# Hymba-style two-layer trunk: the last token tile's second half of y in two 256-column banks, and its reciprocal root by square root on ScalarE and reciprocal on VectorE

## The chip, the cores and the metric

The program runs on one core of a Trainium2 chip. The metric is device microseconds of one execution; lower is better. Three runs of the kernel before took 316.14 to 316.76 us, with a median of 316.38 us. A separate execution was profiled, and its own time is given below.

## The reference

Two layers work on x, which has 256 tokens (two tiles of 128) and 1024 columns. Each layer computes:

```
mod = silu(c) @ W_ada + b_ada                 -> shift, scale, gate
h   = RMSNorm(x) * (1 + scale) + shift
[q k v g for branch A | q k v g for branch B] = h @ W_in
o_A = dilated sliding-window attention,  o_B = block-sparse attention
y   = RMSNorm([o_A*silu(g_A) | o_B*silu(g_B)] @ W_out)
x   = x + gate * y
```

RMSNorm divides each token's row by the root of its mean square plus 1e-6. So the last thing that the program does, for each token tile of the second layer, is: multiply by W_out, take the mean square over 1024 columns, form its reciprocal root, scale, add to x, and write 128 rows of the result.

## The kernel before

Every float32 operand of a product is split in two parts: a rounded high part (tiles `whi`, `hi`) and the rest (`wlo`, `lo`). A product is then three matrix multiplications: high by high, low by high and high by low. Weights stream from HBM in pieces of 512 KB into a ring of seven buffers (`raw`). ScalarE makes `whi` from a piece (line 205), VectorE makes `wlo` (line 212, one instruction for each 512 columns), and TensorE multiplies with `product` (line 513: 512 columns of weights move past 128 tokens).

The first 60 us or so are a list of steps in a fixed order (`FIRST_STEPS`), which interleaves the first layer's modulation (its weights are multiplied directly, line 414, and the result leaves by line 418), the first norm (lines 702 and 713), the first input products (line 753) and the tables of sines and cosines (`make_rope`, lines 328 to 331). A step `w00` splits one weight piece on ScalarE and VectorE, the step `s00` right behind it multiplies with it, and then `a2` and `b2` multiply modulation weights. After this list only TensorE keeps the order in which the code is written (line 836). The order of the other engines' instructions is chosen by a scheduler, from what each instruction depends on; it may place an instruction ahead of code that stands earlier. Within one engine the queue is then worked off in order.

ScalarE's functions come from tables. Where an instruction needs a function that the loaded table does not hold, an `ACT_TABLE_LOAD` stands in its queue. Square and Copy need none of their own in this program: they run behind Silu, Sin and Exp without one.

The end of a layer for one token tile is `out_product` (which calls `product` for each half `cc` of the 1024 columns and each branch `br`) and `post_norm`. In the last layer's last tile the half `cc` = 0 is finished first (both branches), then `cc` = 1 gets branch 0 and branch 1: 24 matrix multiplications with 512 columns into one PSUM bank. `post_norm` squares each half on ScalarE with a running sum (line 685: an ACTIVATE and a read of the accumulator), multiplies it by the gate on VectorE (line 687), adds the two sums and epsilon on GpSimd (line 464) and raises the sum to the power -0.5 there (line 465). VectorE then scales and adds x for both halves (line 691), and SyncE issues a write for each (line 693).

Of the kernel before, what the change touches and what calls it, by code (L numbers as in the profile page):

```python
# [9 lines left out]
F32 = mybir.dt.float32  # L10
F32R = mybir.dt.float32r
I32 = mybir.dt.int32
AF = mybir.ActivationFunctionType
ALU = mybir.AluOpType
PSUM = bass.MemoryType.PSUM

P = 128
# [3 lines left out]
EPS = 1e-6  # L21
# [53 lines left out]
def trunk(ctx: ExitStack, tc: tile.TileContext, x, c, positions, pre_gain, post_gain,  # L75
          w_ada, b_ada, w_in, w_out, out):
    nc = tc.nc
    B, S, DM = x.shape
    L = w_in.shape[0]
    KT = DM // P  # L80
    KH = KT // 2
    NT = S // P
    CW = 512
# [6 lines left out]
    ap = ctx.enter_context(tc.tile_pool(name="acts", bufs=1))  # L90
    ps = ctx.enter_context(tc.tile_pool(name="psum", bufs=1, space=PSUM))
    start = ExitStack()
# [7 lines left out]
    xs = ap.tile([P, NT, DM], F32, name="xs")  # L100
# [67 lines left out]
    for x in FIRST_LOADS.split():  # L168
        i, g, m = x[0], int(x[1]), int(x[2:] or 0)
        if i in "ab":  # L170
            n = GROUPS[g][1]
# [24 lines left out]
    hi_q, lo_q = {}, {}  # L196
# [25 lines left out]
    ones = cp.tile([P, P], F32, name="ones")  # L222
# [3 lines left out]
    dummy = cp.tile([P, 1], F32, name="dummy")  # L226
# [152 lines left out]
    def ada_sum(l):  # L379

        assert all((l, i) in folded for i in range(KT))
        pm = ps.tile([P, CW], F32, name="o", bufs=1)
        for j in range(4):
            nc.tensor.matmul(pm[32 * j:32 * j + 32, :], ones[:, 0:32], acc[l, 0][:, j * CW:(j + 1) * CW],
                             start=True, stop=True, tile_position=(0, 32 * j))
        part = ap.tile([P, CW], F32, name="hf", bufs=2)
        nc.scalar.activation(part, pm, AF.Copy)
        parts[l] = part

    parts = {}  # L390
# [39 lines left out]
    gate = {}  # L430
# [24 lines left out]
        nc.vector.tensor_mul(gate[l][:, sl], pm, gate[l][:, sl])  # L455


    def rstd_of(ms, other=None):

        e = ap.tile([P, 2], F32, name="rstd", bufs=4)  # L460
        if other is None:
            nc.gpsimd.tensor_scalar(e[:, 0:1], ms, EPS, None, op0=ALU.add)
        else:
            nc.gpsimd.tensor_scalar(e[:, 0:1], ms, other, EPS, op0=ALU.add, op1=ALU.add)
        nc.gpsimd.tensor_tensor(e[:, 1:2], e[:, 0:1], nhalf, op=ALU.pow)
        return e[:, 1:2]
# [9 lines left out]
    def pre_norm(l, t):  # L476
        xn = ap.tile([P, DM], F32, name="oo", bufs=2)
        ms = ap.tile([P, 2], F32, name="ms", bufs=4)
        for cc in range(2):
            sl = slice(cc * CW, (cc + 1) * CW)  # L480
            nc.scalar.activation(xn[:, sl], xs[:, t, sl], AF.Square, scale=1.0 / 32.0, accum_out=ms[:, cc:cc + 1])
        r = rstd_of(ms[:, 0:1], ms[:, 1:2])
        nc.scalar.activation(xn[:, 0:CW], xs[:, t, 0:CW], AF.Copy, scale=r)
        nc.vector.tensor_scalar_mul(xn[:, CW:DM], xs[:, t, CW:DM], r)
        return xn
# [19 lines left out]
    def product(bank, act, t, key, first, last, part=None):  # L505

        if key + (0 if part is None else part,) not in hi_q:
            split_upto(seq.index(key) + 1)
        ahi, alo = act
        for k in range(KH) if part is None else (2 * part, 2 * part + 1):  # L510
            whi, wlo = hi_q[key + (k // 2,)], lo_q[key + (k // 2,)]
            for i, (a, w) in enumerate(((ahi, whi), (alo, whi), (ahi, wlo))):
                nc.tensor.matmul(bank, a[:, k, t, :], w[:, k % 2, :], start=first and k + i == 0,  # L513
                                 stop=last and k == KH - 1 and i == 2)
# [16 lines left out]
    qk, vv, gs, qkT, oo = {}, {}, {}, {}, {}  # L531
# [120 lines left out]
    oT = {}  # L652
# [19 lines left out]
    yb = {}  # L672

    def out_product(l, t, cc, br):
        if br == 0:
            yb[t, cc] = ps.tile([P, CW], F32, name="mm", bufs=3)
        assert ready_o[br] == KH
        product(yb[t, cc], oT[br], t, ("out", l, cc, br), br == 0, br == 1)

    def post_norm(l, t, last):  # L680
        ms = ap.tile([P, 4], F32, name="ms2", bufs=2)
        sq = ap.tile([P, NT, CW], F32, name="qk", bufs=3)[:, 0, :]
        yg = ap.tile([P, DM], F32, name="oo", bufs=2)
        for cc in range(2):
            nc.scalar.activation(sq, yb[t, cc], AF.Square, scale=1.0 / 32.0, accum_out=ms[:, cc:cc + 1])  # L685
            sl = slice(cc * CW, (cc + 1) * CW)
            nc.vector.tensor_mul(yg[:, sl], yb.pop((t, cc)), gate[l][:, sl])  # L687
        r = rstd_of(ms[:, 0:1], ms[:, 1:2])
        for cc in range(2):
            sl = slice(cc * CW, (cc + 1) * CW)  # L690
            nc.vector.scalar_tensor_tensor(xs[:, t, sl], yg[:, sl], r, xs[:, t, sl], op0=ALU.mult, op1=ALU.add)
            if last:
                nc.sync.dma_start(out[0, t * P:(t + 1) * P, sl], xs[:, t, sl])
# [75 lines left out]
    def sub_in(l, ci, hf, t, part=None):  # L769
        if l == 0 and part is not None:  # L770
            ready(t, 4 * hf + 2 * part + 1)
        begin = hf == 0 or (l, ci) == (0, 5) and len(parked) > 0
        if (l, ci, t) not in mm:
            tag = "mm" if (l, ci) != (0, 2) else ("s", "t")[t]
            mm[l, ci, t] = ps.tile([P, CW], F32, name=tag, bufs=3 if tag == "mm" else 2)
        if CH[ci] % 4 == 3:
            gate_product(mm[l, ci, t], hT[l, hf], t, ("in", l, ci, hf), hf)
        else:
            product(mm[l, ci, t], hT[l, hf], t, ("in", l, ci, hf), begin, hf == 1, part)
        if hf == 1 and part != 0:  # L780
            evac(l, ci, t)

    seq = list(loads)
    spl = [0]

    def split_upto(n):
        while spl[0] < min(n, len(seq)):
            split_half(seq[spl[0]])
            for a in ADA_AT.get(spl[0], []):
                ada_step(a)  # L790
            spl[0] += 1
# [9 lines left out]
    for step in FIRST_STEPS.split():  # L801
        i, g, m = step[0], int(step[1]), int(step[2:] or 0)
# [38 lines left out]
    for l in range(L):  # L841
        nxt = l + 1 < L
        slots = []
        if l > 0:
            slots += [(0, 0, 0), (0, 1, 0), (1, 0, 0), (1, 1, 0), (0, 0, 1), (0, 1, 1), (1, 0, 1), (1, 1, 1)]
        for ci in range(2, 8):
            if l > 0 or ci != 2 and not (ci == 5 and parked):
                slots += [(ci, 0, 0), (ci, 0, 1)]
            slots += [(ci, 1, 0), (ci, 1, 1)]
        side = {}  # L850

        def at(i, f, *a):
            side.setdefault(i, []).append((f, a))
        for p in range(4):
            for br, o in ((0, AT_A[l]), (1, AT_B[l])):
                d = OS[l], OX[l], OV[l]
                at(o + 2 * p, st_T, br, p)
                at(o + d[0] + 2 * p, st_S, br, p)
                at(o + d[1] + 2 * p, st_X, br, p)
                at(o + d[2] + 2 * p, st_V, br, p)  # L860
        for p in range(4):
            at(AO[l] + AO2[l] * p // 2, finish, 0, p)
        at(GATE_AT[l], gate_begin, l)
        for h in range(2):
            at(GATE_AT[l] + GATE_D[l] + h, gate_end, l, h)
        if l > 0:
            for g in range(2):
                at(H_AT[g], make_h, l, 1, xn0[1], (g,))
        for n, (ci, hf, t) in enumerate(slots):
            i = n + 32 - len(slots)  # L870
            split_upto(seq.index(("in", l, ci, hf)) + AHEAD[l])
            sub_in(l, ci, hf, t)
            for f, a in side.get(i, []):
                f(*a)
        base = seq.index(("out", l, 0, 0))
        split_upto(base + 2)
        out_product(l, 0, 0, 0)
        for i in range(32, 42):
            for f, a in side.get(i, []):
                f(*a)  # L880
        out_product(l, 0, 1, 0)
        split_upto(base + 4)
        if nxt:
            ada_sum(l + 1)
        out_product(l, 0, 0, 1)
        if nxt:
            ada_mod(l + 1)
        out_product(l, 0, 1, 1)
        post_norm(l, 0, not nxt)
        if nxt:  # L890
            xn0[0] = pre_norm(l + 1, 0)
        for cc, br in (((0, 0), (1, 0), (0, 1)) if nxt else ((0, 0), (0, 1), (1, 0))):
            out_product(l, 1, cc, br)
        if nxt:
            split_upto(base + 6)
            make_h(l + 1, 0, xn0[0])
        out_product(l, 1, 1, 1)
        post_norm(l, 1, not nxt)
        if nxt:
            xn0[1] = pre_norm(l + 1, 1)  # L900


# [26 lines left out]
```

## Time and profile before

| What | Value |
| --- | --- |
| Runs, median (lowest to highest) | 316.38 us (316.14 to 316.76) |
| Profiled execution: own time, span | 316.34 us, 314.3 us |
| TensorE, share of the span | 94% |
| VectorE, ScalarE, GpSimd | 78%, 65%, 4% |
| Granted TensorE clock, mean over the span | 0.997 of full speed |

The span runs from the first to the last profiled instruction, so 2.04 us of the profiled execution lie outside it. Busy shares are means over stages with different limits. The chain of waits follows the work that ended last back to the start, and says for each moment which engine the end was waiting for. In the rows, PE is TensorE, PEld its weight load, ACT ScalarE, DVE VectorE, POOL GpSimd and SP SyncE; a q behind a name is that engine's sequencer.

### The profile page before, as it was taken

What the parts mean: (1) busy time and instruction counts of PE and PEld (TensorE: products, weight loads), DVE (VectorE), ACT (ScalarE), POOL (GpSimd) and SP (SyncE); (2) the same over time, 40 slices, a digit from 0 to 9 for tenths busy, and PEclk for the clock granted to TensorE, in tenths of its full rate; (3) what the DMA queues carried; (4) which work ended last, traced back from release to release, by engine and by line L of the source; (5) the groups of instructions that cost most, each with busy time, mean ns of one, the idle gap of its engine ahead of it and who ended that gap; (6) DMA issues with size and microseconds to landing.
All of it is one profiled execution on the core that took longest, in us unless ns stands there. A gap on an engine that the chain in (4) does not pass through costs nothing.

```text
span 314.3 us, 5293 instructions
## 1 busy us (share of the span) xinstructions
PE 295.7 (94%) x1817; PEld 237.5 (76%) x1817; DVE 245.4 (78%) x637; ACT 203.9 (65%) x435; POOL 12.4 (4%) x46
## 2 busy tenths in 40 slices
PE   0889999989999999999999999999999999999992
PEld 0666576868777799997787788777777799997881
DVE  4775974999999999989589999979965566776122
ACT  3645363969597569988387385598775579984100
POOL 3100001000010000000021200000000000000001
PEclk9999999999999999999999999999999999999998
DMA  7999999999888877787937649987844441000011
GB/s 248 339 360 355 346 349 283 325 375 302 286 284 291 291 262 246 211 282 242 325 133 232 217 154 340 341 317 239 252 150 136 136 137 64 2 1 2 0 67 67
DMA packets 37394, 70.63 MB, mean 225 GB/s; under 512 B 2492, under 2 KB 12790, under 8 KB 37368
## 3 DMA queue, kind: packets, MB, share of 16 engines
q1 hardware_dynamic: 36960, 69.22, 65.8%
q10 hardware_dynamic: 408, 1.09, 0.9%
q8 instruction: 14, 0.23, 0.3%
q14 instruction: 12, 0.10, 0.1%
HBM read 69.24 MB, written 1.05 MB: 224 GB/s over the span
## 4 chain that ended last, share of the span: by engine, by line
PE 83%; DVE 5%; DMA 4%; ACT 3%; issue 1%; POOL 1%; SPq 1%; ACTq 0%; DVEq 0%; POOLq 0%
PE mm L513 41%; PE mm L526 15%; PE o L642 4%; PE mm L753 4%; PE t L625 4%; PE t L513 3%; DVE wlo L212 2%; PE t L571 2%; DMA raw<-in_w_ada_dram 2%; PE o L414 2%; PE s L592 2%; PE s L595 2%; DMA rows<-in_b_ada_dram 2%; PE s L753 1%; ACT whi L205 1%
## 5 line engine op out<-in xcount | busy, mean ns | idle before, releaser
L212 DVE TENSOR_TENSOR wlo<-raw,whi 128x512 fp32r<-128x512 f32 x160 | 102.3, 688 | 6.5 <-PE mm L513 3.6
L205 ACT ACTIVATE whi<-raw 128x1024 fp32r<-128x1024 f32 (+1 forms) x88 | 84.2, 979 | 24.8 <-DMA raw<-in_w_in_dram 10.5
L513 PE MATMUL mm<-whi,hi 128*128 128x512 f32 x200 | 81.7, 408 | 0.0
L513 PE MATMUL mm<-wlo,hi 128*128 128x512 f32 x200 | 79.1, 395 | 0.0
L513 PE MATMUL mm<-whi,lo 128*128 128x512 f32 x200 | 79.0, 395 | 0.0
L513 PEld LDWEIGHTS mm<-whi,hi 128*128 128x128 f32 x200 | 37.6, 188 | 10.4 <-issue 1.7
L513 PEld LDWEIGHTS mm<-wlo,hi 128*128 128x128 f32 x200 | 37.6, 188 | 8.8
L513 PEld LDWEIGHTS mm<-whi,lo 128*128 128x128 f32 x200 | 37.7, 189 | 8.1 <-DVE lo L502 0.3
L526 PE MATMUL mm<-hi,whi 128*128 128x256 f32 x128 | 37.2, 291 | 0.0
L526 PE MATMUL mm<-hi,wlo 128*128 128x256 f32 x128 | 36.1, 282 | 0.0
L526 PE MATMUL mm<-lo,whi 128*128 128x256 f32 x128 | 36.0, 281 | 0.0
L604 ACT ACTIVATE z<-z,den 128x128 f32<-128x128 f32 x64 | 28.3, 447 | 5.0 <-DVE den L601 4.9
L526 PEld LDWEIGHTS mm<-hi,whi 128*128 128x128 f32 x128 | 24.1, 188 | 1.2 <-issue 0.2
L526 PEld LDWEIGHTS mm<-lo,whi 128*128 128x128 f32 x128 | 24.2, 189 | 0.2
L526 PEld LDWEIGHTS mm<-hi,wlo 128*128 128x128 f32 x128 | 24.1, 188 | 0.0
L364 DVE SCALAR_TENSOR_TENSOR acc_g<-raw,cs,acc_g 128x1024 f32<-128x1024 f32 x16 | 20.6, 1284 | 2.8 <-DMA raw<-in_w_ada_dram 2.7
L687 DVE TENSOR_TENSOR oo<-mm,gate 128x512 f32<-128x512 f32 x8 | 5.5, 690 | 17.8 <-ACT qk L685 17.7
L685 ACT ACTIVATE qk<-mm 128x512 f32<-128x512 f32 x8 | 4.7, 592 | 21.9 <-PE mm L513 21.9
L364 DVE SCALAR_TENSOR_TENSOR acc_ss<-raw,cs,acc_ss 128x1024 f32<-128x1024 f32 x14 | 17.6, 1275 | 0.0
L628 ACT ACTIVATE pT<-t 128x384 f32<-128x384 f32 x32 | 14.0, 493 | 0.1
L642 PE MATMUL o<-pT,vv 128*64 128x128 f32 x192 | 14.0, 281 | 0.0
L625 PE MATMUL t<-ident,z 128*128 128x128 f32 x96 | 13.6, 277 | 0.0
(173 smaller groups left out, 450.6 us busy)
## 6 DMA issues: line engine op xcount, KB each, us to landing
raw<-in_w_in_dram SPq DMA_DIRECT2D x64, 512.0 KB, 5.3
raw<-in_w_ada_dram SPq DMA_DIRECT2D x32, 512.0 KB, 5.0
raw<-in_w_ada_dram SPq DMA_DIRECT2D x32, 256.0 KB, 6.0
raw<-in_w_out_dram SPq DMA_DIRECT2D x16, 512.0 KB, 4.9
xs<-in_x_dram SPq DMA_DIRECT2D x2, 512.0 KB, 4.3
gate<-in_post_norm_gain_dram ACTq DMA_DIRECT2D x2, 512.0 KB, 5.2
out_dram<-xs SPq DMA_DIRECT2D x4, 256.0 KB, 2.1
rows<-in_b_ada_dram ACTq DMA_DIRECT2D x2, 8.0 KB, 5.3
```

The lines of the kernel that those rows point to most:

```text
L205: nc.scalar.activation(hi_q[key][:, a:b, :], raw[:, a:b, :], AF.Copy)
L212: nc.vector.tensor_sub(lo[:, d, :], raw[:, d, :], hi[:, d, :].bitcast(F32))
L364: nc.vector.scalar_tensor_tensor(a[:, sl], r[:, sl], cs[:, k:k + 1], a[:, sl], op0=ALU.mult, op1=ALU.add)
L414: nc.tensor.matmul(pm[32 * j:32 * j + 32, :w], csz[:, k, :], r[:, i * w:(i + 1) * w], start=k < 4, stop=k >= 4, tile_position=(0, 32 * j))
L513: nc.tensor.matmul(bank, a[:, k, t, :], w[:, k % 2, :], start=first and k + i == 0, stop=last and k == KH - 1 and i == 2)
L526: nc.tensor.matmul(bank[:, b * S:(b + 1) * S], w[:, k % 2, c0:c0 + P], a[:, k].rearrange("p t q -> p (t q)"), start=hf + b + k + i == 0, s ...
L571: nc.tensor.transpose(pt[:, (2 * i + t) * P:(2 * i + t + 1) * P], qk[br, i][:, t, p * P:(p + 1) * P], ident)
L604: nc.scalar.activation(z[:, a:b], z[:, a:b], AF.Exp, bias=den[:, 0, t, i:i + 1], scale=-1.0, accum_out=den[:, 1, t, i:i + 1])
L625: nc.tensor.transpose(pt[:, b * P:(b + 1) * P], pp[i][:, b * P:(b + 1) * P], ident)
L628: nc.scalar.activation(d, pt[:, :NS], AF.Copy)
L642: nc.tensor.matmul(ob[i * HD:(i + 1) * HD, q0:q0 + P], v[:, t, h], res[i][:, c0:c0 + P], start=t == 0, stop=n != 1, tile_position=(0, i * HD))
L753: nc.tensor.matmul(mm[0, ci, t], a[:, k, t, :], w[:, ci, :], start=q == 0 and j == 0 and i == 0, stop=q == 3 and j == 1 and i == 2)
```

## The change

Only the last token tile of the last layer is touched. Its second half of y goes to two PSUM banks of 256 columns each (`last_product`), by 48 matrix multiplications with 256 columns in place of 24 with 512; the first 256 columns are complete 12 multiplications ahead of the others. `last_norm` squares and gates three parts (512, 256 and 256 columns). GpSimd adds the first two sums and then epsilon; ScalarE takes the square root of the third sum with this as its bias; VectorE forms the reciprocal. The power on GpSimd goes. A square root of a constant into a tile that nothing reads (`dummy`) stands ahead of the squares in the code.

```diff
-    def rstd_of(ms, other=None):
+    def rstd_of(ms, other=None, last=False):
-        e = ap.tile([P, 2], F32, name="rstd", bufs=4)
+        e = ap.tile([P, 3], F32, name="rstd", bufs=4)
+        if last:
+            nc.gpsimd.tensor_scalar(e[:, 0:1], ms, EPS, None, op0=ALU.add)
+            nc.scalar.activation(e[:, 2:3], other, AF.Sqrt, bias=e[:, 0:1])
+            nc.vector.reciprocal(e[:, 1:2], e[:, 2:3])
+            return e[:, 1:2]
...
+    def last_product(l, t, br):
+        if br == 0:
+            yb[t, 1] = [ps.tile([P, CW], F32, name="s", bufs=2) for _ in range(2)]
...
+        for c in range(2):
+            for k in range(KH):
+                whi, wlo = hi_q[key + (k // 2,)], lo_q[key + (k // 2,)]
+                for i, (a, w) in enumerate(((ahi, whi), (alo, whi), (ahi, wlo))):
+                    nc.tensor.matmul(yb[t, 1][c][:, :H], a[:, k, t, :], w[:, k % 2, c * H:(c + 1) * H],
+                                     start=br + k + i == 0, stop=br == 1 and k == KH - 1 and i == 2)
...
+    def last_norm(l, t):
...
+        parts = [(yb[t, 0], 0, CW), (yb[t, 1][0][:, :H], CW, CW + H), (yb[t, 1][1][:, :H], CW + H, DM)]
+        nc.scalar.activation(dummy, ones[:, 0:1], AF.Sqrt)
+        for n, (y, a, b) in enumerate(parts):
+            nc.scalar.activation(sq[:, 0:b - a], y, AF.Square, scale=1.0 / 32.0, accum_out=ms[:, n:n + 1])
+            nc.vector.tensor_mul(yg[:, a:b], y, gate[l][:, a:b])
+            if n == 1:
+                nc.gpsimd.tensor_tensor(ms[:, 3:4], ms[:, 0:1], ms[:, 1:2], op=ALU.add)
+        r = rstd_of(ms[:, 3:4], ms[:, 2:3], True)
+        for cc in range(2):
+            sl = slice(cc * CW, (cc + 1) * CW)
+            nc.vector.scalar_tensor_tensor(xs[:, t, sl], yg[:, sl], r, xs[:, t, sl], op0=ALU.mult, op1=ALU.add)
+            nc.sync.dma_start(out[0, t * P:(t + 1) * P, sl], xs[:, t, sl])
```

The queues show where the scheduler put the new instructions. Lines behind the inserted code have higher numbers in the changed kernel: 702, 713 and 726 are 743, 754 and 767 there. First ScalarE's queue near the start of the program, before: the second tile's first norm (`acc_ss`), the copies of transposed x, then a modulated part of h (`hi`), the sines and cosines, and the weight piece of step `w00` (128x1024).

```order
L702 ACTIVATE acc_ss,ms<-xs 128x1024
L713 ACTIVATE acc_g<-t 128x512 x2
...
L726 ACTIVATE hi<-hf 128x128 x2
L328 ACTIVATE sine<-sm 128x2x8
L329 ACTIVATE sine<-sm 128x2x8
L330 ACTIVATE cose<-sm 128x2x8
L331 ACTIVATE cose<-sm 128x2x8
L205 ACTIVATE whi<-raw 128x1024
```

The same two places now:

```order
L743 ACTIVATE acc_ss,ms<-xs 128x1024
L709 ACT_TABLE_LOAD
L709 ACTIVATE dummy<-ones 128x1
L754 ACTIVATE acc_g<-t 128x512 x2
...
L767 ACTIVATE hi<-hf 128x128 x2
L328 ACT_TABLE_LOAD
L328 ACTIVATE sine<-sm 128x2x8
L329 ACTIVATE sine<-sm 128x2x8
L330 ACTIVATE cose<-sm 128x2x8
L331 ACTIVATE cose<-sm 128x2x8
L205 ACTIVATE whi<-raw 128x1024
```

The square root of the constant depends on nothing but a constant, and stands at the start of the program instead of ahead of the last squares. It brings a table load, and the sines and cosines behind it bring another.

Then the end of ScalarE's queue, before: the last attention output and the four squares of the two tiles.

```order
L667 ACTIVATE hi<-oo 128x256 [waits DVE_49]
L685 ACTIVATE qk,ms_3517<-mm 128x512 [waits PE_49]
L685 ACTIVATE qk,ms_3517<-mm 128x512 [waits PE_49,Activation_49]
L685 ACTIVATE qk,ms_3581<-mm 128x512 [waits PE_49]
L685 ACTIVATE qk,ms_3581<-mm 128x512 [waits PE_49,Activation_49]
```

The same place now:

```order
L726 ACTIVATE qk,ms_3517<-mm 128x512 [waits PE_49,Activation_49]
L711 ACTIVATE qk,ms_3606<-mm 128x512 [waits PE_49]
L711 ACTIVATE qk,ms_3606<-s 128x256 [waits PE_49,Activation_49] x2
L463 ACT_TABLE_LOAD [waits Activation_49]
L463 ACTIVATE rstd<-ms_3606,rstd 128x1 [waits Pool_49]
```

Behind the last square there is now a table load, and then the square root. On VectorE a reciprocal of 128x1 follows, ahead of the two last additions; and one weight split in the first layer's attention changes places with its neighbours.

## Rows read from the trace of the kernel before

**Rows 1.** The page: shares of the chain of waits by engine.

```profile
PE 83%; DVE 5%; DMA 4%; ACT 3%; issue 1%; POOL 1%; SPq 1%; ACTq 0%; DVEq 0%; POOLq 0%
```

**Rows 2.** Chain of waits, its end: start us, us, what.

```profile
288.26 19.81 PE mm L513 x84
...
308.16 0.60 ACT qk L685
...
308.94 0.30 POOL rstd L464
...
309.92 0.75 DVE xs L691
```

**Rows 3.** Timeline, the end: start us, us, engine, line, operation [idle before it].

```profile
307.66 0.40 PE L513 MATMUL mm<-wlo,hi 128*128 128x512 f32 x1
...
308.65 0.19 ACT L685 ACTIVATION_READ_ACCUMULATOR qk<-mm 128x1 f32 x1
308.88 0.69 DVE L687 TENSOR_TENSOR oo<-mm,gate 128x512 f32<-128x512 f32 x1 [4.97 <-ACT qk L685]
...
309.32 0.56 POOL L465 TENSOR_TENSOR rstd<-rstd,nhalf 128x1 f32<-128x1 f32 x1
```

**Rows 4.** Chain of waits, unbroken runs of 512-column and of 256-column multiplications.

```profile
237.51 5.58 PE mm L513 x24
...
277.30 5.76 PE mm L526 x48
```

**Rows 5.** Groups by line and form: busy us, mean ns of one, idle before.

```profile
L561 ACT ACT_TABLE_LOAD x4 | 5.1, 1283 | 0.1
L650 ACT ACTIVATE oo<-o 128x256 f32<-128x256 f32 x13 | 4.9, 378 | 0.1
L685 ACT ACTIVATE qk<-mm 128x512 f32<-128x512 f32 x8 | 4.7, 592 | 21.9 <-PE mm L513 21.9
L608 DVE RECIPROCAL rc<-den 128x4 f32<-128x4 f32 x16 | 2.8, 175 | 4.2 <-ACT z L604 4.2
```

**Rows 6.** Timeline, ScalarE around a table load.

```profile
280.16 0.51 ACT L612 ACTIVATE z<-z,rc 128x256 f32<-128x256 f32 x1 [0.25 <-DVE rc L608]
280.69 1.28 ACT L561 ACT_TABLE_LOAD   x1
281.98 0.60 ACT L561 ACTIVATE gs<-mm 128x512 f32<-128x512 f32 x1
```

**Rows 7.** Timeline, ScalarE at the first place near the start.

```profile
9.29 0.19 ACT L702 ACTIVATION_READ_ACCUMULATOR acc_ss<-xs 128x1 f32 x1
10.70 0.60 ACT L713 ACTIVATE acc_g<-t 128x512 f32<-128x512 f32 x1 [1.22 <-PE t L712]
11.55 0.60 ACT L713 ACTIVATE acc_g<-t 128x512 f32<-128x512 f32 x1 [0.26 <-PE t L712]
```

**Rows 8.** Timeline, ScalarE, VectorE and TensorE at the second place near the start.

```profile
18.93 0.57 ACT L726 ACTIVATE hi<-hf 128x128 fp32r<-128x128 f32 x2 [0.54 <-DVE hf L724]
...
19.40 0.20 ACT L328 ACTIVATE sine<-sm 128x16 f32<-128x16 f32 x1
...
19.83 1.04 ACT L205 ACTIVATE whi<-raw 128x1024 fp32r<-128x1024 f32 x1
...
20.28 1.91 DVE L212 TENSOR_TENSOR wlo<-raw,whi 128x512 fp32r<-128x512 f32 x3
...
21.86 0.39 PE L513 MATMUL s<-whi,hi 128*128 128x512 f32 x1
...
23.35 2.32 PE L414 MATMUL o<-raw,csz 128*32 128x512 f32 x16
```

**Rows 9.** Timeline, SyncE: the last loads for those multiplications of line 414.

```profile
16.96 1.00 SPq L136 DMA_DIRECT2D raw<-in_w_ada_dram  x2
```

**Rows 10.** The instructions of line 136: from issue to landing.

```profile
DMA to landing us min/median/max: 4.0/6.0/6.6
```

**Rows 11.** Timeline, TensorE: the same 16 multiplications of the next group.

```profile
47.09 1.92 PE L414 MATMUL o<-raw,csz 128*32 128x512 f32 x16
```

More of the change, by code (lines that the diff above doesn't have):

```diff
@@ L678, in out_product @@
         product(yb[t, cc], oT[br], t, ("out", l, cc, br), br == 0, br == 1)
+    def last_product(l, t, br):
+        if br == 0:
+            yb[t, 1] = [ps.tile([P, CW], F32, name="s", bufs=2) for _ in range(2)]
+        key = ("out", l, 1, br)
+        if key + (0,) not in hi_q:
+            split_upto(seq.index(key) + 1)
+        ahi, alo = oT[br]
+        H = CW // 2
+        for c in range(2):
[5 more added lines that the diff above has]
+    def last_norm(l, t):
+        ms = ap.tile([P, 4], F32, name="ms2", bufs=2)
+        sq = ap.tile([P, NT, CW], F32, name="qk", bufs=3)[:, 0, :]
+        yg = ap.tile([P, DM], F32, name="oo", bufs=2)
+        H = CW // 2
+        parts = [(yb[t, 0], 0, CW), (yb[t, 1][0][:, :H], CW, CW + H), (yb[t, 1][1][:, :H], CW + H, DM)]
[10 more added lines that the diff above has]
+            nc.sync.dma_start(out[0, t * P:(t + 1) * P, sl], xs[:, t, sl])
     def post_norm(l, t, last):
@@ L892, in trunk @@
         for cc, br in (((0, 0), (1, 0), (0, 1)) if nxt else ((0, 0), (0, 1), (1, 0))):
-            out_product(l, 1, cc, br)
+            if nxt or cc == 0:
+                out_product(l, 1, cc, br)
+            else:
+                last_product(l, 1, br)
         if nxt:
@@ L896, in trunk @@
             make_h(l + 1, 0, xn0[0])
-        out_product(l, 1, 1, 1)
-        post_norm(l, 1, not nxt)
-        if nxt:
+            out_product(l, 1, 1, 1)
+            post_norm(l, 1, False)
             xn0[1] = pre_norm(l + 1, 1)
+        else:
+            last_product(l, 1, 1)
+            last_norm(l, 1)
 _INS = ["x", "c", "positions", "pre_norm_gain", "post_norm_gain", "w_ada", "b_ada", "w_in", "w_out"]
```

## The prediction

> **What bounds the kernel now.** I read the page's shares of the chain of waits first. TensorE holds 83% of it, and no other engine more than 5% [rows 1]; so what delays TensorE anywhere delays the end, unless a later wait swallows it. Then I read the end of the chain: 84 multiplications in an unbroken run from 288.26 us, then the square on ScalarE at 308.16, the two instructions on GpSimd from 308.94, and VectorE's scaling at 309.92 [rows 2]. Everything between TensorE's last multiplication, which ends at 307.66 + 0.40 = 308.06 [rows 3], and 309.92 stands alone on the path: 1.86 us in which one engine works at a time. That is what the change rebuilds. What lies behind 309.92 (two additions, two writes) is the same in both kernels. Third I read the timeline at the places near the start where the queue shows new table loads, because there too the reader is to ask who waits behind ScalarE.
>
> **The end, part by part.** The 24 multiplications with 512 columns become 48 with 256. An unbroken run of 24 with 512 columns took 5.58 us and one of 48 with 256 columns, elsewhere in the kernel, 5.76 us [rows 4]. So TensorE ends 0.18 later, at 308.24.
>
> ScalarE started its square 0.10 behind TensorE's end (308.06 to 308.16), and I keep that: 308.34. The square of 512 columns and its accumulator read were over at 308.65 + 0.19 = 308.84, which is 0.68 behind its start [rows 2, 3]. No square of 256 columns is in the trace. From PSUM, a copy of 256 columns took 378 ns and the square of 512 took 592 ns [rows 5]; I take the difference, 0.21, off: the third square is done at 308.34 + 0.47 = 308.81. The bounds are the square of 512 unchanged (0.68) and the copy without any read behind it (0.38).
>
> Now comes the table load of the square root. It stands behind the last square in a queue that is worked off in order, and it waits for that square itself, so nothing covers it. The one at 280.69 began 0.02 behind the end of the instruction ahead of it, took 1.28, and the next instruction began 0.01 later [rows 6]; the mean of its group is 1283 ns [rows 5]. So it runs from 308.83 to 310.11. The square root of 128x1 is not in the trace either; a sine of 128x16 took 0.20 [rows 8], and I take that: 310.12 to 310.32. Its bounds are that 0.20 and the 0.38 of the copy of 256 columns. VectorE starts 0.04 behind ScalarE (308.84 to 308.88 [rows 3]): 310.36. A reciprocal of 128x4 took 175 ns [rows 5], and with 0.03 to the next instruction VectorE scales at 310.56, against 309.92 before: 0.64 later.
>
> Of the work that was taken out, the power on GpSimd (0.56 [rows 3]) and the sum ahead of it (0.30 [rows 2]) go from the path. GpSimd's two new sums need only the first two squares. The middle square starts when the first 256 columns are ready, 12 multiplications or 1.44 us ahead of the end (12 of 5.76 / 48), at about 306.9, and is done at 307.4; two sums of 0.30 with gaps of 0.1 are over by 308.2, long before the square root wants them at 310.1. VectorE's product with the gate for the last 256 columns starts when the third square is done, as the one at 308.88 did [rows 3], and at no more than the 0.69 of 512 columns ends by 309.6; it is covered too. Without the load the same sum would end at 309.27, 0.65 earlier than before: the load alone turns a gain into a loss.
>
> Here a page of the Trainium skill bears: "ScalarE: Activation LUTs", section "What ACT_TABLE_LOAD costs", gives 1283 ns for the load, which the rows share, and about as much again for a drain at each switch, 2.66 us in all. The trace has no such second part beside the load at 280.69; by the page the sum of the end would be near 2.0 us later instead of 0.64. I leave it as a rival below.
>
> **The start, part by part.** The square root of a constant was placed at the start. Its load falls behind the accumulator read that ends at 9.48, where ScalarE was idle for 1.22 us until 10.70 [rows 7]. Load and dummy: 9.50 to 10.78, then about 0.1 to 0.2 for the dummy, so the copy that began at 10.70 begins near 10.9. The next copy waited for TensorE until 11.55 with 0.26 of idle time ahead of it [rows 7], and still starts then. This place costs nothing: the cover is ScalarE's own wait.
>
> The second place is tighter. The sines need their table again, and the load starts behind the pair that ends at 18.93 + 0.57 = 19.50 [rows 8]: 19.52 to 20.80, first sine 20.81 instead of 19.40, all behind it 1.41 later. Behind it stands the split of the weight piece of step `w00`: it ran from 19.83 to 20.87, now from 21.24 to 22.28. TensorE wanted it at 21.86 [rows 8], so 0.99 of the delay is covered and the first of six multiplications starts near 22.32. Its third and sixth also need VectorE's two splits of that piece. The three splits from 20.28 took 1.91 [rows 8], so one follows the other by 0.61 and the last lasts 0.69; now the two start at 22.31 and 22.92 and end at 22.99 and 23.61. At 0.233 for each multiplication (5.58 / 24) the six start at 22.32, 22.55, 23.03, 23.26, 23.50 and 23.73; the sixth stood at 21.86 + 5 x 0.233 = 23.02 before. TensorE is 0.71 late.
>
> Part of that is given back at once. The 16 multiplications of line 414 that follow took 2.32 us from 23.35 [rows 8], and the same 16 of the next group 1.92 [rows 11]: 0.40 of the first was a wait for weights. The last two loads were issued between 16.96 and 17.96 [rows 9], and such a load lands 6.0 us after its issue in the median [rows 10], at 23.0 to 24.0. Starting at 23.35 + 0.71 = 24.06, TensorE finds them there: 24.06 + 1.92 = 25.98 against 23.35 + 2.32 = 25.67. I take 0.31 late. From there on the chain is TensorE behind TensorE, or an engine that waits for TensorE, and I see no wait that gives it back.
>
> SyncE's queue is behind this too: the buffer of that weight piece comes free 1.4 later, and so does the load that waits for it. The loads already issued keep the DMA engines busy meanwhile, so I take nothing for it. The bounds of the start are 0 (a later wait for weights swallows the rest) and 1.41 (the late loads pass the whole delay on).
>
> The exchange of one weight split with its neighbours on VectorE changes no sum of work; I take 0, with 0.1 either way.
>
> **Sum.** The profiled execution took 316.34 us, of which 314.3 was span: 316.34 + 0.64 + 0.31 = 317.29, that is 317.3. The median of the runs is 316.38, so about 0.9 us or 0.3% slower.
>
> **The rivals.**
>
> 1. The start costs nothing in the end: a wait for weights that I can't see in TensorE's chain takes up the 0.31. Time 316.34 + 0.64 = 316.98. For it: such a wait already takes 0.40 of the 0.71. Against it: behind 25.67 the chain hardly leaves TensorE.
>
> 2. The delay of the start is passed on in full, through the buffer that comes free late. Between 0.71 and 1.41 instead of 0.31: 317.7 to 318.4. For it: a load is issued only when a buffer of the ring is free. Against it: a load lands 6 us after its issue, so several are on their way at any time.
>
> 3. The other side, not slower: the load at the end is hidden, because ScalarE fetches the table while it waits for TensorE ahead of the last square. Then the end gains 0.65 and the time is 316.34 - 0.65 + 0.31 = 316.0, or 315.7 with nothing lost at the start. It decides from the point where more than half of the 1.28 is hidden. For it: ScalarE is idle most of the last 20 us. Against it: the load waits for the square itself, and the load at 280.69 started behind the instruction ahead of it and not earlier [rows 6].
>
> 4. A switch of tables costs twice its load, as a drain of the same length would make it: 1.28 more at the end and 1.28 more at the second place of the start, where no cover is left: 317.29 + 2.56 = 319.9. The skill's page above has this rule. Against it: no gap of that size stands around the load at 280.69 [rows 6].
>
> **How the numbers follow.** The forecast has 58%, rival 1 18%, rival 2 13%, rival 3 8% (5% at 316.0, 3% at 315.7), rival 4 3%. A measurement of this kernel can tell about 0.2% from no change, 0.63 us: slower is above 317.01, faster below 315.75. The forecast's own range is 317.2 to 317.7 (the square 0.09 shorter or 0.21 longer, the root up to 0.18 longer). With rival 1 and the lower half of rival 2 the range is 316.8 to 317.9. Slower: 58 + 13 + 3 = 74%; same: 18 + 5 = 23%; faster: 3%. Since the forecast lies only 0.28 above the bound of slower, I move two points, one to each of the others: 72, 24 and 4%.
>
> **What would show it.** At the end of the changed profile: a table load of 1.28 directly behind the last accumulator read, on the chain of waits, and the first scaling some 2.3 us behind TensorE's last multiplication instead of 1.86. At the start: the second load near 19.5, the first multiplication of `s00` near 22.3, and the 16 of line 414 in about 1.9 instead of 2.32, ended near 26.0. TensorE's last multiplication then ends about 0.49 later than before, 0.31 from the start and 0.18 from the narrower tiles. I am wrong if the load is missing from the chain, and the start is wrong if that end is no later than the 0.18 of the narrower tiles.

## The result, and the profile after

| | Median (lowest to highest), runs | Profiled execution, span |
| --- | --- | --- |
| Before | 316.64 us (316.14 to 316.76), 6 | 316.34 us, 314.3 us |
| After | 318.50 us (317.39 to 319.34), 6 | 318.35 us, 316.3 us |

The ratio is 1.0058, with a 95% interval of 1.0045 to 1.0072: slower by 1.4 to 2.3 us. The forecast was slower by 0.95 us, 317.3 in a range that ended at 317.9. The direction was right, the size about half.

**The end.** This is the end of the chain of waits after, which answers to [rows 2] (start us, us, what).

```profile
303.77 5.71 PE s L698 x48
...
309.56 0.48 ACT qk L711 x2
...
310.12 1.28 ACT L463
311.40 0.32 ACTq L970
...
311.94 0.75 DVE xs L718
```

The table load stands on the chain, whole. And these are TensorE, ScalarE, VectorE and GpSimd in the timeline of the same stretch after, which answers to [rows 3] (start us, us, engine, line, operation, and in brackets the idle time before it).

```profile
308.98 0.22 POOL L462 TENSOR_SCALAR rstd<-ms 128x1 f32<-128x1 f32 x1
...
309.19 0.28 PE L698 MATMUL s<-wlo,hi 128*128 128x256 f32 x1
309.56 0.38 ACT L711 ACTIVATE qk<-s 128x256 f32<-128x256 f32 x1 [0.95 <-PE s L698]
309.85 0.19 ACT L711 ACTIVATION_READ_ACCUMULATOR qk<-s 128x1 f32 x1
310.07 0.43 DVE L712 TENSOR_TENSOR oo<-s,gate 128x256 f32<-128x256 f32 x1 [1.00 <-ACT qk L711]
310.12 1.28 ACT L463 ACT_TABLE_LOAD   x1
311.41 0.29 ACT L463 ACTIVATE rstd<-ms,rstd 128x1 f32<-128x1 f32 x1
311.74 0.16 DVE L464 RECIPROCAL rstd<-rstd 128x1 f32<-128x1 f32 x1 [1.24 <-ACT rstd L463]
```

GpSimd has the sum ready by 309.20 (308.98 + 0.22) and VectorE the gated product by 310.50, but the root runs at 311.41 only, behind the load. TensorE's last multiplication ends at 309.47 (309.19 + 0.28) and VectorE scales at 311.94: 2.47 us, against 1.86 before.

**The start.** ScalarE after, at the place of [rows 7].

```profile
8.70 0.19 ACT L743 ACTIVATION_READ_ACCUMULATOR acc_ss<-xs 128x1 f32 x1
8.91 1.28 ACT L709 ACT_TABLE_LOAD   x1
10.20 0.20 ACT L709 ACTIVATE dummy<-ones 128x1 f32<-128x1 f32 x1
10.31 1.25 ACT L754 ACTIVATE acc_g<-t 128x512 f32<-128x512 f32 x2
```

This execution is ahead of the one before here (the read stood at 9.29), since TensorE's first transposition (line 275), which in the kernel before waits for a load, began at 7.32 here and at 7.90 there. So times near the start must be read against their spread: in the seven profiles in which the ring has seven buffers and the split of `w00` is on time, the first 16 multiplications of line 414 end between 25.03 and 25.67, and the next 16 between 48.73 and 49.33. ScalarE and TensorE after, at the place of [rows 8]:

```profile
18.82 0.57 ACT L767 ACTIVATE hi<-hf 128x128 fp32r<-128x128 f32 x2 [0.84 <-DVE hf L765]
19.40 1.28 ACT L328 ACT_TABLE_LOAD   x1
20.70 0.22 ACT L328 ACTIVATE sine<-sm 128x16 f32<-128x16 f32 x1
...
21.14 1.04 ACT L205 ACTIVATE whi<-raw 128x1024 fp32r<-128x1024 f32 x1
...
22.23 0.50 PE L518 MATMUL s<-whi,hi 128*128 128x512 f32 x1 [0.62 <-ACT whi L205]
...
24.09 1.92 PE L414 MATMUL o<-raw,csz 128*32 128x512 f32 x16
```

The 16 multiplications take 1.92 instead of 2.32 and end at 26.01 instead of 25.67 [rows 8]: 0.34 late, as the prediction had it (0.31). But by the end of the next group of 16 [rows 11], at 49.97 instead of 49.01, the delay is 0.96. It grows between, at the next eight multiplications of line 414. TensorE there before, and after:

```profile
32.51 1.12 PE L414 MATMUL o<-raw,csz 128*32 128x512 f32 x8
```

```profile
32.95 1.65 PE L414 MATMUL o<-raw,csz 128*32 128x512 f32 x8
```

SyncE's queue shows what came late. The load of line 126 goes into the buffer of the piece that step `w00` splits. SyncE before, and after:

```profile
22.26 0.34 SPq L126 DMA_DIRECT2D raw<-in_w_in_dram  x1
24.44 0.37 SPq L121 DMA_DIRECT2D raw<-in_w_in_dram  x1
24.91 2.64 SPq L136 DMA_DIRECT2D raw<-in_w_ada_dram  x4
```

```profile
23.57 0.34 SPq L126 DMA_DIRECT2D raw<-in_w_in_dram  x1
25.18 0.37 SPq L121 DMA_DIRECT2D raw<-in_w_in_dram  x1
25.65 1.76 SPq L136 DMA_DIRECT2D raw<-in_w_ada_dram  x2
```

That load is issued 1.31 later, and the loads behind it in the queue, which bring the weights of line 414, 0.74 later. The DMA view of the stretch from 20 to 30 us says whether the loads issued earlier covered that, before and after:

```profile
DMA packets 2354, 3.59 MB, mean 359 GB/s; under 512 B 151, under 2 KB 1584, under 8 KB 2352
```

```profile
DMA packets 1937, 3.18 MB, mean 318 GB/s; under 512 B 130, under 2 KB 1167, under 8 KB 1935
```

They did not: 0.41 MB fewer were moved in the same 10 us, which at 359 GB/s is 1.1 us of transfers. Most of it is missing in two microseconds: from 26 to 28 us the DMA engines moved 0.39 MB, against 0.70 before.

**The middle.** One more difference lies at the boundary of the layers, where GpSimd adds epsilon for the second tile and VectorE waits for the result. GpSimd and VectorE in the timeline before, then after:

```profile
173.97 2.49 DVE L212 TENSOR_TENSOR wlo<-raw,whi 128x512 fp32r<-128x512 f32 x4
...
174.91 1.04 POOL L464 TENSOR_SCALAR rstd<-ms 128x1 f32<-128x1 f32 x1 [2.30 <-ACT oo L481]
...
176.91 0.48 DVE L484 TENSOR_SCALAR oo<-xs,rstd 128x512 f32<-128x512 f32 x1 [0.45 <-POOL rstd L465]
```

```profile
174.96 2.50 DVE L212 TENSOR_TENSOR wlo<-raw,whi 128x512 fp32r<-128x512 f32 x4
...
175.90 1.72 POOL L469 TENSOR_SCALAR rstd<-ms 128x1 f32<-128x1 f32 x1 [2.31 <-ACT oo L486]
...
178.30 0.49 DVE L489 TENSOR_SCALAR oo<-xs,rstd 128x512 f32<-128x512 f32 x1 [0.85 <-POOL rstd L470]
```

The same instruction, begun 0.94 behind the start of VectorE's four splits in both, lasts 1.04 in one and 1.72 in the other. VectorE goes on 1.39 late (176.91 to 178.30), 0.43 more than the 0.96 of the start.

**The ledger of the two profiles.** 0.34 at the start, 0.62 from there to 34 us, 0.43 at the layers' boundary, 0.10 for the narrower tiles (48 with 256 columns in 5.71 us, 24 with 512 in 5.6), and 0.61 behind TensorE make 2.10; the spans differ by 2.0, and some 0.07 is given back between the boundary and the last product.

### The profile page after: what moved, and what is told of

The parts are those of the page before. It is cut to its first block, busy times and chain, and to the rows that moved or that the text cites. A ratio compares the mean times of both kernels' runs of the same rounds, so it can differ in the third digit from the quotient of the medians.

```text
span 316.3 us, 5351 instructions
## 1 busy us (share of the span) xinstructions
PE 297.5 (94%) x1841; PEld 238.9 (76%) x1841; DVE 245.8 (78%) x639; ACT 208.5 (66%) x442; POOL 12.4 (4%) x46
## 4 chain that ended last, share of the span: by engine, by line
PE 84%; DVE 6%; ACT 5%; issue 2%; POOL 1%; ACTq 1%; DVEq 0%; POOLq 0%
PE mm L518 39%; PE mm L531 15%; PE o L647 4%; PE t L630 4%; DVE wlo L212 3%; PE mm L794 3%; PE t L518 3%; PE o L414 3%; PE t L576 2%; PE s L597 2%; PE s L698 2%; PE s L600 2%; ACT whi L205 1%; PE s L518 1%; PE s L794 1%
## 5 line engine op out<-in xcount | busy, mean ns | idle before, releaser
L518 PE MATMUL mm<-whi,hi 128*128 128x512 f32 x192 | 78.5, 409 | 0.0
L518 PE MATMUL mm<-wlo,hi 128*128 128x512 f32 x192 | 75.9, 395 | 0.0
L518 PE MATMUL mm<-whi,lo 128*128 128x512 f32 x192 | 75.8, 395 | 0.0
L518 PEld LDWEIGHTS mm<-whi,hi 128*128 128x128 f32 x192 | 36.1, 188 | 10.1 <-issue 1.7
L518 PEld LDWEIGHTS mm<-wlo,hi 128*128 128x128 f32 x192 | 36.1, 188 | 8.4
L518 PEld LDWEIGHTS mm<-whi,lo 128*128 128x128 f32 x192 | 36.2, 189 | 7.7 <-DVE lo L507 0.3
L647 PEld LDWEIGHTS o<-pT,vv 128*64 128x64 f32 x192 | 10.1, 136 | 4.3 <-issue 2.0
L584 DVE TENSOR_TENSOR qkl<-t,qkh 128x384 fp32r<-128x384 f32 x16 | 8.9, 555 | 5.1 <-ACT qkT L583 4.9
```

The source lines that it names most:

```text
L584: nc.vector.tensor_sub(lo, pt[:, P:], hi.bitcast(F32))
L647: nc.tensor.matmul(ob[i * HD:(i + 1) * HD, q0:q0 + P], v[:, t, h], res[i][:, c0:c0 + P], start=t == 0, stop=n != 1, tile_position=(0, i * HD))
```

## The experiments

The theory, A in the texts: the end costs what was forecast, and the start costs more, because the split of `w00` stands behind a table load and its buffer comes free late, so that loads queued on SyncE come late (A1 where that part of A is meant alone). The rivals are told in the texts with their numbers: that the end or the table loads themselves cost more than forecast, wherever they stand. Each ratio is to the kernel before on the same chip.

### The end without the early load

```diff
-        nc.scalar.activation(dummy, ones[:, 0:1], AF.Sqrt)
```

> The change without its idle square root near the start: no table load there, the load at the end stays. Theory A (the excess over the forecast arises at the start, passed on by late weight loads): only the end is left, 0.6 to 0.75 us over before, about 317.3 us. Theory B (the load at the end costs more than its 1.28 us): the end holds most of the 1.85, about 318.1 us or more.

Measured: 316.78 us against 316.24, ratio 1.0019 (1.0007 to 1.0031), some 0.6 us. The end is the same as in the changed kernel, 2.47 us behind TensorE's last multiplication, and the 16 and 8 multiplications of line 414 take 2.26 and 1.15, as before. So the rebuilt end costs about 0.6 us, and the rest of the loss hangs on the line that was taken out.

### The early load alone, in the kernel before

```diff
+        if last and t == 1:
+            nc.scalar.activation(dummy, ones[:, 0:1], AF.Sqrt)
```

> The kernel before with nothing but the idle square root of a constant: two table loads near the start, the end as it was. Theory A: 1.0 to 1.3 us over before, about 317.8 us, with TensorE waiting for weights of line 414 near 33 us. Theory B: 0.3 us over before, about 316.9 us.

Measured: 317.94 us against 316.24, ratio 1.0043 (1.0021 to 1.0066), 1.36 us by the ratio (0.66 to 2.09), which leaves out theory B's 0.3. A load of a table that no one uses at the start, with nothing changed at the end (1.86 us), costs more than the whole new end. The timeline of its TensorE shows the wait openly:

```profile
33.38 1.05 PE L414 MATMUL o<-raw,csz 128*32 128x512 f32 x4
34.81 1.05 PE L414 MATMUL o<-raw,csz 128*32 128x512 f32 x4 [0.37 <-DMA raw<-in_w_ada_dram]
```

and the list of what its weight loads waited for between 30 and 36 us (us in total, times, longest) names the load:

```profile
PEld o L414 <- DMA raw<-in_w_ada_dram: 1.3, 1, 1.3
```

Its SyncE issued the load of line 126 at 24.04 and those of line 136 from 26.11, and from 20 to 30 us it moved 3.01 MB. The two parts add up within their intervals: 0.60 and 1.36 make 1.96, against 1.84 by the ratio of the first comparison and 2.09 by that of the next run.

### The changed kernel once more

No edit.

> The changed kernel once more, for a second profile and more times: its six times spread over 1.95 us, those of before over 0.62. Theory A: about 318.5 us in the median with the same spread, and the profile shows the delay differing from the first one's between 20 and 50 us and at the layers' boundary, while the end (first scaling 2.46 us behind TensorE's last multiplication) is the same to 0.05. Theory B: the end differs.

Measured: 318.37 us against 316.24, ratio 1.0066 (1.0044 to 1.0088). The loss repeats, and the end is 2.47 again. In this profile the eight multiplications of line 414 took 2.09 (32.73 to 34.82) instead of the 1.65 above: how long TensorE waits there varies from one execution to the next, and the runs of the changed kernel spread over 2 us. The list of waits from 30 to 36 us names the load here too; for the 1.65 above it names nothing ("issue", 0.8 us in two pieces).

```profile
PEld o L414 <- DMA raw<-in_w_ada_dram: 0.9, 1, 0.9
```

### The warm-up held back to the last squares

The square root of a constant becomes one of the first square's sum, so that it cannot be placed before it; its load then stands between the first square and the second.

```diff
-        nc.scalar.activation(dummy, ones[:, 0:1], AF.Sqrt)
...
             nc.vector.tensor_mul(yg[:, a:b], y, gate[l][:, a:b])
+            if n == 0:
+                nc.scalar.activation(dummy, ms[:, 0:1], AF.Sqrt)
```

> The change with the idle square root fed by the first square's sum, so that its load stands between the first and the second square, where ScalarE is idle for some 4 us. Both theories: no load at the start, the one at the end covered; the first scaling 1.15 us behind TensorE's last multiplication instead of 2.46, and 0.55 to 0.65 us under before, about 316.0 us. If a load could not be covered, 317.3 us as without the idle square root.

Measured: 315.84 us against 316.24, ratio 0.9987 (0.9973 to 1.0001). The first scaling comes 1.19 us behind TensorE's last multiplication. Both parts of the loss are gone with one line; the interval just reaches no change, so it was run again below.

### The sines behind the split

The steps `w00` and `s00` are moved ahead of `R2`, which holds the sines. All table loads stay.

```diff
-g02 R2 l11 g03 p02 w00 s00 a2 b2 m2
+g02 l11 g03 p02 w00 s00 R2 a2 b2 m2
```

> The changed kernel with the step of the sines (R2) moved behind steps w00 and s00, so that the second table load of the start runs in ScalarE's idle time. All table loads stay. Theory A (the start's cost comes from the split of w00 that stands behind that load): the start is as before and only the end is left, 0.55 us over before, about 316.8 us; TensorE reaches the first multiplication of s00 near 21.9 us. Theory C (the cost comes from the first of the two loads, or from their number): about 1.9 us over before, as the changed kernel.

Measured: 317.04 us against 316.49, ratio 1.0016 (1.0006 to 1.0027). ScalarE now has the split first and the load behind it:

```profile
19.40 1.05 ACT L205 ACTIVATE whi<-raw 128x1024 fp32r<-128x1024 f32 x1
20.47 1.28 ACT L328 ACT_TABLE_LOAD   x1
```

SyncE issues line 126 at 22.23 as before (22.26), and the eight multiplications take 1.06. Of the loss, only what the kernel without the early load also has is left (1.0019 there). So a load near the start costs nothing that these intervals, some 0.5 us wide to either side, can show where the split does not stand behind it: theory C, by which the loads cost by themselves (1.9 us), falls. The run does not tell TensorE's direct delay from the late loads; the ring below does.

### Two banks, the power kept

The early load goes, and GpSimd forms the reciprocal root by power as before.

```diff
-        nc.scalar.activation(dummy, ones[:, 0:1], AF.Sqrt)
...
-        r = rstd_of(ms[:, 3:4], ms[:, 2:3], True)
+        r = rstd_of(ms[:, 3:4], ms[:, 2:3])
```

> The change with its two banks and three squares, but with the power on GpSimd as before and no square root. Forecast from the parts measured: TensorE 0.10 later, square and accumulator read 0.20 shorter: the first scaling 1.65 us behind TensorE's last multiplication, about 0.1 us under before. If a third square or the two banks cost by themselves: 0.2 us or more over before.

Measured: 316.55 us against 316.49, ratio 0.9997 (0.9987 to 1.0006). The scaling comes 1.70 behind TensorE, 0.16 less than before, and the narrower tiles cost 0.10: no change that can be told, as the sum says. The long form of GpSimd's instruction at the layers' boundary appears here too, without any early load:

```profile
175.23 1.72 POOL L469 TENSOR_SCALAR rstd<-ms 128x1 f32<-128x1 f32 x1 [2.31 <-ACT oo L486]
```

### One bank, the root on ScalarE, its load covered

The last tile keeps one bank of 512 columns; square root and reciprocal as changed; the warm-up behind the first square.

```diff
-        parts = [(yb[t, 0], 0, CW), (yb[t, 1][0][:, :H], CW, CW + H), (yb[t, 1][1][:, :H], CW + H, DM)]
+        parts = [(yb[t, 0], 0, CW), (yb[t, 1], CW, DM)]
...
-        r = rstd_of(ms[:, 3:4], ms[:, 2:3], True)
+        r = rstd_of(ms[:, 0:1], ms[:, 1:2], True)
```

> One bank of 512 columns as before, but square root on ScalarE and reciprocal on VectorE, with the table load covered behind the first square. TensorE as before; square and read 0.68, root 0.30, reciprocal 0.20 and the gaps: the first scaling 1.35 us behind TensorE's last multiplication instead of 1.86, about 0.5 us under before. If root and reciprocal without a load were worth nothing: equal to before.

Measured: 316.31 us against 316.49, ratio 0.9994 (0.9982 to 1.0007). The tail is 1.55 us, and the expectation missed it by 0.20. The end of its chain of waits names what it left out:

```profile
308.22 0.70 ACT qk L710 x2
...
308.94 0.69 DVE oo L711
309.63 0.08 DVE rstd L464
...
309.74 0.75 DVE xs L717
```

VectorE's product with the gate, over 512 columns, stands in its queue ahead of the reciprocal and ends behind the root. It was covered by the two GpSimd instructions before; with a shorter root it is what ends last. The second bank shortens it (0.43 for 256 columns), so the two halves of the change are worth more together: in the profiles 0.06 and 0.31 alone, and 0.58 together in the last run below.

### One buffer more in the ring

Eight `raw` buffers in place of seven, paid for with one `whi` buffer. First the kernel before with this ring:

```diff
-NRAW, NHI, NLO = (7, 9, 8)
+NRAW, NHI, NLO = (8, 8, 8)
```

> The kernel before with eight buffers for weight pieces instead of seven (and eight instead of nine for their high parts, for the space): the control of the next run. No theory says more than that it stays within 1 us of before.

Measured: 319.41 us against 316.38, ratio 1.0107 (1.0070 to 1.0143). The control is not neutral, as it was expected to be; it is 3 us slower. In its profile TensorE was idle for 1.83 us, until 126.84, for a result of VectorE (line 579), which it does not wait for in the kernel before. Behind that the granted clock over 125 to 135 us was 0.83 of full speed in the mean, so a part of that stretch stood at the lower of the two levels (1.2 of 2.4 GHz): the 15 multiplications with 256 columns from 128.10 took 3.36 us, where 15 of 48 in 5.76 [rows 4] would be 1.80. The next kernel, just as slow, waits for the same line for 1.8 us in all, with a mean clock of 0.997 over its span. At the end of the second group of 16 multiplications of line 414 both kernels stand where the kernel before does (48.77 and 49.09, against 49.01), so the 3 us arise behind the stretch that is read here; their cause is open, and the totals of these two kernels are of little use.

Then the same ring with the early load of the second experiment:

> The same with the idle square root and so the two table loads near the start. With seven buffers that cost 1.4 to 1.7 us. With eight, the buffer of w00 is awaited by a load that comes later in the queue. Theory A1 (TensorE's direct delay is the smaller part, and late loads, which wait for that buffer, the larger): 0.3 to 0.8 us over its control, and the eight multiplications of line 414 near 33 us take about as long as in the control. Theory A2 (the direct delay is all): 1.4 us or more over its control.

Measured: 319.66 us against 316.38, ratio 1.0108 (1.0081 to 1.0136), so 0.25 us over its own control by the medians and 0.03 by the ratios, where the same early load cost 1.36 with seven buffers. Each ratio is known to about 1 us only, so the totals don't decide between the theories, and the rows before 50 us have to. The table load delays the split as much as ever, and the buffer's next load (now a line 121) is issued 1.44 later, at 23.12 instead of 21.68. But TensorE does not wait longer for it: it took 1.21 us for the eight, and 1.48 in the control.

```profile
32.48 1.21 PE L414 MATMUL o<-raw,csz 128*32 128x512 f32 x8
```

And its DMA engines, from 20 to 30 us, moved as much as without the early load (3.74 MB in both kernels of this ring):

```profile
DMA packets 2511, 3.74 MB, mean 374 GB/s; under 512 B 166, under 2 KB 1741, under 8 KB 2509
```

By the end of the next group of 16 it was 0.32 late against its control (49.09 and 48.77), no more than the direct delay; the early load with seven buffers stood at 51.25 there. Over all profiles with seven buffers this one row splits cleanly: 3.59 to 3.72 MB in the seven in which the split is on time, 3.01 to 3.18 MB in the three in which it is late.

The length of the eight multiplications does not split so. In three of the seven profiles with the split on time TensorE waits there too (1.52, 1.57 and 1.94 us), the longest with the two banks and the power kept:

```profile
32.01 1.94 PE L414 MATMUL o<-raw,csz 128*32 128x512 f32 x8
```

TensorE comes early there (at 31.90 to 32.08) and waits; for what, the list of waits does not name. What splits is when the eight are over: 33.37 to 33.95 with the split on time, 34.60 to 35.86 with the split late.

### The better version once more

The kernel with the warm-up held back, unchanged.

> The change with its idle square root fed by the first square's sum, once more, for a narrower interval: its first profile had the first scaling 1.19 us behind TensorE's last multiplication instead of 1.86, and TensorE 0.1 later from the narrower tiles, so 0.5 to 0.6 us under before, about 0.2%. If the noise of the loads hides it: within 0.1% of before.

Measured: 315.37 us (315.22 to 316.14, 10 runs) against 316.38, ratio 0.9970 (0.9958 to 0.9981): 0.95 us faster than the kernel before, more than expected. The end of its chain of waits:

```profile
302.15 5.71 PE s L698 x48
...
307.94 0.48 ACT qk L710 x2
...
308.45 0.43 DVE oo L711
308.88 0.14 DVE rstd L464
...
309.03 0.75 DVE xs L719
```

TensorE ends at 307.85, so the scaling at 309.03 is 1.18 behind it instead of 1.86. Less 0.10 for the narrower tiles, the end gains about 0.58; the rest of the 0.95 lies inside the intervals of the two comparisons (0.9973 to 0.9981 is in both).

## Why the prediction was right or wrong

**The end: right.** Forecast 0.64 later; in the profile 0.71, of which 0.61 behind TensorE and 0.10 for the narrower tiles; alone on the chip about 0.6 (0.2 to 1.0). The load took 1.28, stood behind the last square and was covered by nothing, as the sum had it. Three terms were off and nearly cancelled, which is luck: the narrower tiles 0.10 instead of 0.18; the square with its read done 0.48 behind its start instead of 0.47, but 0.08 before the load instead of 0.02; the root 0.29 instead of 0.20. The nearest row, a sine of 128x16, has no tile as bias. The dummy root of 128x1, which has none either, took 0.20 too, and the one with GpSimd's sum as bias 0.29. The Trainium skill, "ScalarE: Activation LUTs", section "What ACT_TABLE_LOAD costs", states about 93 ns for each such operand; these two rows agree.

**The table load counted twice (rival 4): refuted.** Between the last read's end (310.04) and the load lies 0.08, behind it 0.01; at the start it is 0.01 to 0.02 on either side. The same section of the Trainium skill states a drain of about 1380 ns for each switch; these rows do not agree with it, since no gap beside a load is longer than 0.08.

**The load fetched ahead while ScalarE waits (rival 3): refuted.** ScalarE was idle for 0.95 before the last square, and the load still began behind it. But what rival 3 would have given, 315.7 to 316.0, is about what the kernel gives whose load is made to stand ahead of the second square by the code (315.37 and 315.84).

**The first place near the start: right.** The load at 8.91 lay in ScalarE's wait; with the split out of the way of the second load, the early loads cost nothing that the intervals can show.

**The direct delay of the second place: right.** 0.34 at the end of the 16 multiplications, where 0.31 was forecast, with the 0.40 of waiting for weights given back. The other two profiles with a late split end there at 25.82 and 26.47; against 25.03 to 25.67 with the split on time this agrees, but no finer than some 0.3 us. Counted from where ScalarE comes to the sines or to the load before them (19.40 in both kernels here), it is finer: that end lies 6.59 to 6.61 behind in the four profiles with a late split, the ring of eight among them, and 6.15 to 6.27 in six of the seven that have the sines ahead of a split on time. In the seventh, one of the kernel with the warm-up held back, it is 5.57; there too the 16 took 1.92.

**The step that failed** is the sentence on SyncE's queue: "The loads already issued keep the DMA engines busy meanwhile, so I take nothing for it." They did not. The buffer came free 1.31 later; SyncE, which works its queue off in order, could issue nothing behind the load that waited for it; 0.4 to 0.6 MB less was moved from 20 to 30 us, and at about 33.5 us TensorE stood and waited for weights, some 0.5 us longer than before in one profile of the changed kernel, 1.0 in the other, 1.3 in the early load alone. That took the start from the 0.31 of the forecast to 0.96 in the profile and to 1.36 (0.66 to 2.09) in the timed runs of the early load alone; TensorE's last multiplication ended 1.41 later, where 0.49 was forecast. This is rival 2, to which I had given 13% and a price of 0.71 to 1.41, and it is how the time left the range. The range was also drawn too short by its own words: it was to hold rival 2's lower half, 317.7 to 318.05, and ended at 317.9. The 318.50 lies above both. The row that spoke for rival 2 was in the trace before: the DMA engines' share in that stretch. From 20 to 30 us they moved 359 GB/s, and no slice of the page shows more than 375 (single microseconds of that stretch reach 401), so there was little slack in which a late load could be made up. Rival 1, by which a later wait for weights takes the delay up, falls too: the later wait grew.

**Not in the prediction, and not due to the change as far as the runs tell:** the 0.43 at the layers' boundary. The long form was in the profiles of the changed kernel and in three others, two of them without an early load near the start; the short one in the rest. In the profiled execution it is a second part of the excess over 317.3, beside the 0.65 that the start cost above its 0.31. In the timed runs it need not be: the end alone (0.60) and the early load alone (1.36), both with the short form in their profiles, make up the loss without it, and the kernel with two banks and the power kept, with the long form in its profile, is no slower than before by more than 0.19 us (upper bound 1.0006), where 0.43 in every run, less the 0.06 gained, would be 0.37.

## What to carry to other kernels

A warm-up that depends on nothing late belongs to the scheduler: give it an operand that is made where you want it, or it lands where its side effect (here the next function's table load) hurts. When an instruction that frees a ring buffer becomes late, don't stop at its direct reader: find the load that waits for the buffer, count the loads queued behind it, and compare the bytes moved in that stretch with what the DMA engines could move; if they were busy throughout, the delay can come back as a wait for weights one load's flight later. And when an operation is taken off the end, list everything that it had covered, since the longest of that is what ends last next.

## What the runs showed of the hardware

The same GpSimd instruction on 128x1 (epsilon added to the mean square) took 0.30 us beside VectorE's product with the gate, which has one input from PSUM (before, at 308.94 and 308.88), and longer beside VectorE's splits. At the layers' boundary it took 0.81 to 0.82 for the first tile in every profile, and for the second tile either 1.04 or 1.72 beside four splits, though it began 0.94 behind their start in both cases. In the long case it ended 0.16 behind the last of the splits (177.62 and 177.46), as it did for the first tile, in the short one 0.09 behind the third (175.95 and 175.86). Every profile shows one of these two values for the second tile and nothing between; what decides is open. The Trainium skill, "GPSIMD Engine Reference", section "1. Specifications", says that GpSimd shares its interfaces to SBUF with VectorE and contends with VectorE's instructions that have two inputs from SBUF. The splits are such instructions and the product with the gate is not, so the longer values and the 0.30 agree with it; how long the wait is, and that it has two sizes, that row does not say.

A ring with one buffer more, and one `whi` buffer less, cost 3 us in place of leaving the time as it was; which of the two did it was not tried apart.
